# Softmax gradient with a one-hot label: single rows in four buffers against blocks of two rows in three

## The chip, the cores and the metric

The kernel runs on one core of a Trainium2 chip; the other cores stand idle. The metric is the device time of one execution in microseconds. Before the change it is 1255.14 us, the median of 3 runs (1254.55 to 1255.56).

The core's engines that matter here are the Vector engine (DVE), ScalarE (ACT), GpSimd (POOL) and SyncE (SP). ScalarE and SyncE also issue transfers; each has a hardware queue of its own, and all transfers run on the same 16 DMA engines.

## The reference

Logits are 8 x 1024 rows of 8192 fp32 values, labels one integer for each row. The output has the shape of the logits: the softmax of each row, less 1 at the place of its label.

```python
logits_max = np.max(logits, axis=-1, keepdims=True)
exp_logits = np.exp(logits - logits_max)
softmax = exp_logits / np.sum(exp_logits, axis=-1, keepdims=True)
...
one_hot[batch_idx, seq_idx, labels] = 1.0
return (softmax - one_hot).astype(np.float32)
```

Everything is read once and written once: 268 MB in and 268 MB out.

## The kernel before

The 8192 rows are cut into 64 row tiles of 128 rows, one row on each partition, 32 KB of fp32 a row. One loop runs over the row tiles, unrolled in Python, and a scheduler orders the instructions on each engine and places the waits. A tile goes through these steps:

- L47: SyncE's queue loads the row tile (4.19 MB) into one of the four buffers of the pool `io`. The load of row tile t+4 waits until the store of row tile t has landed, because it takes the same buffer.
- L50 and L57: GpSimd's queue loads 128 labels, and the Vector engine casts them to fp32.
- L61: ScalarE computes the exponential into a bf16 tile and, in the same instruction, the sum of each row. No row maximum is taken away first; the exponential of the plain logit is used.
- L71: the Vector engine takes the reciprocal of the sum.
- L74: it compares a table of column numbers (`iota_pv`, int16, made once at L41) with the label and multiplies by the sum. The result, bf16, overwrites the first half of the logits' buffer, which the exponential has read.
- L83: it subtracts that from the exponential, in bf16.
- L85: it multiplies by the reciprocal and writes fp32 back into the logits' buffer.
- L87: ScalarE's queue stores the buffer.

Nothing but the four buffers, two bf16 tiles and the order on each queue ties one row tile to the next.

Of the kernel before, what the change touches and what calls it, by code (L numbers as in the profile page):

```python
# [1 line left out]

# [4 lines left out]

P = 128


@with_exitstack
def kernel(
    ctx: ExitStack,
    tc: tile.TileContext,
    logits: bass.AP,
    labels: bass.AP,
    out: bass.AP,
):
    nc = tc.nc  # L20
    fp32 = mybir.dt.float32
    bf16 = mybir.dt.bfloat16
    i16 = mybir.dt.int16

    logits_nv = logits.flatten_outer_dims()
    out_nv = out.flatten_outer_dims()
    labels_n = labels
    while len(labels_n.shape) > 1:
        labels_n = labels_n.rearrange("a b ... -> (a b) ...")

    N, V = logits_nv.shape
    assert N % P == 0, f"N={N} must be a multiple of {P}"
    n_tiles = N // P

    const_pool = ctx.enter_context(tc.tile_pool(name="const", bufs=1))
    io_pool = ctx.enter_context(tc.tile_pool(name="io", bufs=4))
    work_pool = ctx.enter_context(tc.tile_pool(name="work", bufs=2))
    stats_pool = ctx.enter_context(tc.tile_pool(name="stats", bufs=4))

    iota_pv = const_pool.tile([P, V], i16)  # L40
    nc.gpsimd.iota(iota_pv[:, :], [[1, V]], channel_multiplier=0)  # L41

    for ti in range(n_tiles):
        rs = ti * P

        logits_tile = io_pool.tile([P, V], fp32, tag="io")
        nc.sync.dma_start(out=logits_tile[:], in_=logits_nv[rs : rs + P, :])  # L47

        labels_tile = stats_pool.tile([P, 1], labels_n.dtype, tag="labels")
        nc.gpsimd.dma_start(out=labels_tile[:], in_=labels_n[rs : rs + P, None])  # L50

        labels_f32 = stats_pool.tile([P, 1], fp32, tag="labels_f32")
        if mybir.dt.size(labels_n.dtype) == 8:
            labels_i32 = labels_tile.bitcast(mybir.dt.int32)[:, :1]
        else:
            labels_i32 = labels_tile[:]
        nc.vector.tensor_copy(out=labels_f32[:], in_=labels_i32)  # L57

        exp_bf = work_pool.tile([P, V], bf16, tag="exp")
        sum_f32 = stats_pool.tile([P, 1], fp32, tag="sum")  # L60
        nc.scalar.activation(  # L61
            out=exp_bf[:],
            in_=logits_tile[:],
            func=mybir.ActivationFunctionType.Exp,
            bias=0.0,
            scale=1.0,
            accum_out=sum_f32[:],
        )

        recip_sum = stats_pool.tile([P, 1], fp32, tag="recip")  # L70
        nc.vector.reciprocal(out=recip_sum[:], in_=sum_f32[:])  # L71

        ohts_bf = logits_tile.bitcast(bf16)[:, :V]
        nc.vector.tensor_scalar(  # L74
            out=ohts_bf,
            in0=iota_pv[:, :],
            scalar1=labels_f32[:],
            scalar2=sum_f32[:],
            op0=mybir.AluOpType.is_equal,
            op1=mybir.AluOpType.mult,  # L80
        )

        nc.vector.tensor_sub(out=exp_bf[:], in0=exp_bf[:], in1=ohts_bf)  # L83

        nc.vector.tensor_scalar_mul(out=logits_tile[:], in0=exp_bf[:], scalar1=recip_sum[:])  # L85

        nc.scalar.dma_start(out=out_nv[rs : rs + P, :], in_=logits_tile[:])  # L87


# [1 line left out]
_INS = ['logits', 'labels']  # L91
_OUTS = [((8, 1024, 8192), 'float32')]


# [23 lines left out]
```

The softmax here doesn't subtract the row's maximum and nothing guards it: scores larger than these inputs give would overflow.

## Time and profile before

| What | Value |
|---|---|
| Device time, median of 3 runs | 1255.14 us |
| Span of the profiled execution | 1252.6 us |
| Vector engine busy | 732.6 us (58%) |
| ScalarE busy | 457.0 us (36%) |
| GpSimd busy | 253.0 us (20%) |
| Queue of the loads, share of 16 DMA engines | 49.8% |
| Queue of the stores, share of 16 DMA engines | 49.6% |
| Queue of the labels, share of 16 DMA engines | 0.1% |
| Bytes moved, mean rate | 537.01 MB, 429 GB/s |

The span runs from the first to the last instruction of the program in the profiled execution; the device time of the runs lies some 2.5 us above it. Busy times are sums over an engine's own instructions, and instructions that issue a transfer aren't counted as busy. The share of a queue is the time that its packets took, against 16 engines over the whole span. A row of the groups names line, engine, operation, output and input with shapes and count, and then gives total busy time, mean duration in ns, and the idle time of the engine ahead of these instructions with what ended it. In the row of 40 digits each digit stands for one fortieth of the span, and 9 is 90% or more.

### The profile page before, as it was taken

The numbers are of one execution on the slowest core, as the hardware profiler recorded it, in microseconds if no ns is written. First come the engines' busy times: TensorE is split into PE (matmuls) and PEld (weight loads), VectorE is DVE, ScalarE is ACT, GpSimd is POOL, SyncE is SP. The second block draws the span as 40 slices with busy tenths as digits, with TensorE's granted clock in tenths as the row PEclk, the third lists the DMA queues.
The fourth block names the chain that finished last, engine by engine and source line by source line (L and its number), as shares of the span: only waits on it lengthen the run. The fifth ranks groups of instructions, "written<-read, shape, count | busy, mean of one in ns | idle before, by whom it ended". The sixth has DMA issues, their size and how long they took to land.

```text
span 1252.6 us, 992 instructions
## 1 busy us (share of the span) xinstructions
DVE 732.6 (58%) x320; ACT 457.0 (36%) x129; POOL 253.0 (20%) x69
## 2 busy tenths in 40 slices
DVE  3764655746647556465574664755646556465573
ACT  4424244243342433423424334243342432423422
POOL 5322212212122122221221212212222122100000
DMA  9999999999999999999999999999999999999997
GB/s 400 421 435 434 433 428 430 433 436 433 435 430 432 431 433 433 434 434 432 429 432 435 431 434 433 431 432 432 434 433 434 433 429 432 432 434 435 434 433 311
DMA packets 20487, 537.01 MB, mean 429 GB/s; under 512 B 4096, under 2 KB 4096, under 8 KB 4096
## 3 DMA queue, kind: packets, MB, share of 16 engines
q1 hardware_dynamic: 9216, 268.44, 49.8%
q10 hardware_dynamic: 9216, 268.44, 49.6%
q0 software_dynamic: 2048, 0.07, 0.1%
q14 instruction: 7, 0.06, 0.0%
HBM read 268.50 MB, written 268.44 MB: 429 GB/s over the span
## 4 chain that ended last, share of the span: by engine, by line
DMA 71%; DVE 17%; issue 8%; ACT 1%; POOL 1%; ACTq 0%; SPq 0%; PEldq 0%
DMA out_dram<-logits_tile 38%; DMA logits_tile<-in_logits_dram 32%; DVE logits_tile L85 7%; DVE exp_bf L83 7%; DVE logits_tile L74 4%; ACT exp_bf L61 1%; DMA labels_tile<-in_labels_dram 1%; POOL iota_pv L41 1%; ACTq L87 0%; POOL labels_tile L50 0%; DVE labels_f L57 0%; DVE recip_sum L71 0%; SPq L47 0%; ACTq L61 0%; PEldq L113 0%
## 5 line engine op out<-in xcount | busy, mean ns | idle before, releaser
L61 ACT ACTIVATE exp_bf<-logits_tile 128x8192 bf16<-128x8192 f32 x64 | 449.8, 7029 | 771.3 <-DMA logits_tile<-in_logits_dram 757.8
L50 POOL DMA_DIRECT2D labels_tile<-in_labels_dram x64 | 245.9, 3843 | 832.1 <-DVE labels_f L57 830.1
L71 DVE RECIPROCAL recip_sum<-sum_f 128x1 f32<-128x1 f32 x64 | 10.5, 163 | 485.1 <-ACT exp_bf L61 485.1
L85 DVE TENSOR_SCALAR logits_tile<-exp_bf,recip_sum 128x8192 f32<-128x8192 bf16 x64 | 287.1, 4486 | 0.1
L83 DVE TENSOR_TENSOR exp_bf<-exp_bf,logits_tile 128x8192 bf16<-128x8192 bf16 x64 | 283.2, 4425 | 2.2
L74 DVE TENSOR_SCALAR logits_tile<-iota_pv,labels_f,sum_f 128x8192 bf16<-128x8192 int16 x64 | 154.3, 2412 | 0.3 <-issue 0.3
L57 DVE CAST labels_f<-labels_tile 128x1 f32<-128x1 int32 x64 | 9.4, 147 | 20.2 <-DMA labels_tile<-in_labels_dram 20.2
L61 ACT ACTIVATION_READ_ACCUMULATOR exp_bf<-logits_tile 128x1 f32 x64 | 11.9, 186 | 0.0
L41 POOL IOTA iota_pv<- 128x8192 int16 x1 | 6.9, 6944 | 0.4 <-PEq L113 0.4
L61 ACT ACT_TABLE_LOAD x1 | 1.3, 1283 | 0.7 <-PEq L102 0.7
L102 POOL MEMSET const-float32-0.0<- 128x1 f32 x1 | 0.1, 99 | 0.2 <-issue 0.2
L102 POOL MEMSET const-bfloat16-1.0<- 128x1 bf16 x1 | 0.1, 102 | 0.0
L102 POOL MEMSET const-uint8-127<- 128x1 uint8 x1 | 0.1, 102 | 0.0
L102 POOL MEMSET const-float32-1.0<- 128x1 f32 x1 | 0.1, 99 | 0.0
## 6 DMA issues: line engine op xcount, KB each, us to landing
logits_tile<-in_logits_dram SPq DMA_DIRECT2D x64, 4096.0 KB, 27.2
out_dram<-logits_tile ACTq DMA_DIRECT2D x64, 4096.0 KB, 31.3
labels_tile<-in_labels_dram POOLq DMA_DIRECT2D x64, 1.0 KB, 12.7
```

The costliest lines, as they stand in the source:

```text
L41: nc.gpsimd.iota(iota_pv[:, :], [[1, V]], channel_multiplier=0)
L50: nc.gpsimd.dma_start(out=labels_tile[:], in_=labels_n[rs : rs + P, None])
L57: nc.vector.tensor_copy(out=labels_f32[:], in_=labels_i32)
L61: nc.scalar.activation(out=exp_bf[:], in_=logits_tile[:], func=mybir.ActivationFunctionType.Exp, bias=0.0, scale=1.0, accum_out=sum_f32[:],)
L71: nc.vector.reciprocal(out=recip_sum[:], in_=sum_f32[:])
L74: nc.vector.tensor_scalar(out=ohts_bf, in0=iota_pv[:, :], scalar1=labels_f32[:], scalar2=sum_f32[:], op0=mybir.AluOpType.is_equal, op1=myb ...
L83: nc.vector.tensor_sub(out=exp_bf[:], in0=exp_bf[:], in1=ohts_bf)
L85: nc.vector.tensor_scalar_mul(out=logits_tile[:], in0=exp_bf[:], scalar1=recip_sum[:])
L102: nc = _bacc.Bacc("TRN2", target_bir_lowering=False, num_devices=1)
```

## The change

The kernel is written anew around blocks of two neighbouring rows for each partition. Partition p of block b holds rows 256b + 2p and 256b + 2p + 1, which lie side by side in memory, so that a partition's part of a block is one run of 64 KB.

- `SLOTS` is 3 and `G`, the rows of a block on each partition, is 2. Three buffers of a block each (8.39 MB, 64 KB on each partition) replace four buffers of a row tile and the two bf16 tiles. All steps work in place in fp32.
- A block moves as one load and one store. The first and the last block are loaded row by row, and the first three and the last two are stored row by row (`BY_ROW_IN`, `BY_ROW_OUT`).
- The labels of all rows are loaded once, cast, and transposed through the tensor engine into one column for each row tile, once for each half of the vocabulary.
- The row maximum is computed (`row_max`) and goes into the exponential as its bias.
- The multiplication by the reciprocal moves to ScalarE (`normalize`, two halves), and compare and subtract are one Vector instruction for each half (`subtract`).
- The order is written out by hand: in the pass of row t the Vector engine takes the reciprocal of t, the maximum of row t+1 and then the subtraction of row t; ScalarE takes the exponential of t, issues the store of row t−1 (for a block, after its second row), and then normalizes t.

The diff, cut to its core:

```diff
-    io_pool = ctx.enter_context(tc.tile_pool(name="io", bufs=4))
-    work_pool = ctx.enter_context(tc.tile_pool(name="work", bufs=2))
+    io = ctx.enter_context(tc.tile_pool(name="io", bufs=SLOTS))
+    ctx.enter_context(tc.manual_schedule())
...
+    x_b = x_nv.rearrange("(b p j) v -> b p j v", p=P, j=G)
+    o_b = o_nv.rearrange("(b p j) v -> b p j v", p=P, j=G)
...
+    lab_raw = const.tile([B, G * P], labels.dtype)
+    nc.scalar.dma_start(out=lab_raw[:], in_=lab_bp)
...
+    for j in range(G):
+        nc.vector.tensor_copy(out=lab_f[:, j, :], in_=lab32[:, j, :, 0])
+        nc.tensor.transpose(out=lab_ps[:, j, :], in_=lab_f[:, j, :], identity=ident[:])
+    for c in range(C):
+        nc.vector.tensor_scalar_add(out=lab[:, c], in0=lab_ps[:], scalar1=float(-c * HALF))
...
+    def load(b):
+        x = io.tile([P, G, V], fp32, tag="x", name="x")
+        if b in BY_ROW_IN:
+            for j in range(G):
+                nc.sync.dma_start(out=x[:, j, :], in_=x_b[b, :, j, :])
+        else:
+            nc.sync.dma_start(out=x[:], in_=x_b[b])
+        return x
+    def row_max(x):
...
+        nc.vector.tensor_reduce(out=m[:], in_=x[:], axis=mybir.AxisListType.X, op=Alu.max, negate=True)
...
+    def exponent(x, m):
...
+        nc.scalar.activation(out=x[:], in_=x[:], func=Act.Exp, bias=m[:], scale=1.0, accum_out=s[:])
...
+    def normalize(x, r):
+        for c in range(C):
+            xc = x[:, c * HALF : (c + 1) * HALF]
+            nc.scalar.activation(out=xc, in_=xc, func=Act.Copy, bias=0.0, scale=r[:])
+    def subtract(t, x):
+        for c in range(C):
+            xc = x[:, c * HALF : (c + 1) * HALF]
+            nc.vector.scalar_tensor_tensor(
+                out=xc, in0=iota[:], scalar=lab[:, c, t % G, t // G : t // G + 1], in1=xc,
+                op0=Alu.is_equal, op1=Alu.subtract, reverse1=True,
+            )
+    def store(t):
+        b, j = divmod(t, G)
+        if b in BY_ROW_OUT:
+            nc.scalar.dma_start(out=o_b[b, :, j, :], in_=blocks[b][:, j, :])
+        elif j == G - 1:
+            nc.scalar.dma_start(out=o_b[b], in_=blocks[b][:])
+    BY_ROW_IN = (0, B - 1)
+    BY_ROW_OUT = (0, 1, 2, B - 2, B - 1)
...
+    m = row_max(row(0))
+    for t in range(T):
+        s = exponent(row(t), m)
+        r = inverse(s)
+        if t + 1 < T:
+            m = row_max(row(t + 1))
+        if t > 0:
+            store(t - 1)
+        normalize(row(t), r)
+        subtract(t, row(t))
+    store(T - 1)
```

## The prediction

> **What bounds the kernel now.** I read the page from its top: span and DMA row first, then the waits of ScalarE and of SyncE's DMA queue, then the costs of single instructions, and last the places where the DMA engines stand still.
>
> ```profile
> span 1252.6 us, 992 instructions
> DVE 732.6 (58%) x320; ACT 457.0 (36%) x129; POOL 253.0 (20%) x69
> DMA  9999999999999999999999999999999999999997
> GB/s 400 421 435 434 433 428 430 433 436 433 435 430 432 431 433 433 434 434 432 429 432 435 431 434 433 431 432 432 434 433 434 433 429 432 432 434 435 434 433 311
> ```
>
> The engines have room, the 16 DMA engines have none: 537 MB at about 433 GB/s are 1240 of the 1252.6 us. The waits say the same:
>
> ```profile
> ACT exp_bf L61 <- DMA logits_tile<-in_logits_dram: 757.8, 62, 19.2
> SPq L47 <- DMA out_dram<-logits_tile: 1169.6, 60, 50.2
> ```
>
> ScalarE waits for loads, and the load queue waits for stores to free one of the four buffers. That second wait costs nothing now: in the chain of waits a load is issued the moment a store lands, while another load or store still keeps the DMA engines busy.
>
> ```profile
> 619.70 31.99 DMA out_dram<-logits_tile
> 651.69 0.02 SPq L47
> 651.74 26.60 DMA logits_tile<-in_logits_dram
> ```
>
> Prices of single instructions, from the groups:
>
> ```profile
> L61 ACT ACTIVATE exp_bf<-logits_tile 128x8192 bf16<-128x8192 f32 x64 | 449.8, 7029 | 771.3 <-DMA logits_tile<-in_logits_dram 757.8
> L83 DVE TENSOR_TENSOR exp_bf<-exp_bf,logits_tile 128x8192 bf16<-128x8192 bf16 x64 | 283.2, 4425 | 2.2
> ```
>
> Prices of a transfer with nothing beside it. In the stretches (length, busy time of DVE, ACT and POOL, clock, DMA share, GB/s) no byte moves before 1.60 us although the first load is issued at 0.75; loads alone run at 420 to 423, loads and stores mixed at 433; and near the end the DMA share falls to 0.41 and 0.75.
>
> ```profile
> 1.20:1.60 0.40, 0.00 (x0) 0.40 (x1) 0.40 (x1) 1.00 0.00 0
> 1.60:2.00 0.40, 0.00 (x0) 0.40 (x1) 0.40 (x1) 1.00 3.27 901
> 20.00:30.00 10.00, 9.36 (x6) 6.89 (x3) 4.17 (x2) 1.00 1.01 420
> 160.00:320.00 160.00, 94.43 (x43) 58.97 (x18) 34.27 (x8) 1.00 1.00 433
> 1230.00:1240.00 10.00, 9.93 (x3) 0.00 (x0) 0.00 (x0) 1.00 0.41 177
> 1240.00:1253.00 13.00, 0.51 (x1) 0.00 (x0) 0.00 (x0) 1.00 0.75 323
> ```
>
> Issue to landing (min/median/max), first of the loads, then of the stores; the two minima are the first load and the last store, which had the engines to themselves:
>
> ```profile
> DMA to landing us min/median/max: 12.3/27.2/48.4
> DMA to landing us min/median/max: 11.1/31.3/33.5
> ```
>
> A row tile is 4.19 MB, 9.7 us at 433 GB/s. So a lone load costs 2.6 us on top of its bytes and a lone store 1.4.
>
> **What the Trainium skill says.** "DMA: Bandwidth & Descriptors", section Anatomy of one DMA, gives each transfer a fixed cost of about 2.0 us, mostly the receipt of the last write, and says that waits are served by the issuing sequencer, not by the DMA engines; the 2.6 and 1.4 us agree in size. Its section Queues, rings and completion order says that each DMA engine takes turns between queues packet by packet, so a load and a store that run together share about evenly; the equal packet shares of the two queues here (49.8% and 49.6%) fit. Its section Where 436 GB/s comes from puts the ceiling at 435.2 GB/s; 433 in the trace is 0.5% below, which bounds what longer runs can give. "VectorE: DVE Perf Modes", section The perf-mode tier table, has a reduction at one element a cycle in any type and a two-input operation on fp32 likewise.
>
> **The change, part by part.**
>
> *Traffic.* Bytes stay. 64 KB runs for 32 KB ones and one label load for 64: between 0 and 1240 × 0.5% = 6 us less; I take 2.
>
> *Vector engine.* It loses L74, L83, L85, and L57's casts, and gains a row maximum over 8192 fp32 and two fused compare-and-subtract over 4096 (int16 and fp32 in). The trace has neither. L83 makes 8192 elements at two a cycle in 4.425 us; at one a cycle 4096 elements cost the same, 4.43, and 8192 cost 8.69 (L83 plus 4096 more cycles at 0.96 GHz, 4.27 us). A row: 8.69 + 2 × 4.43 + 0.16 (reciprocal) = 17.7 us, a block of two rows 35.4, against 38.75 for a block's traffic (16.78 MB at 433). Below: the fused operation can't be cheaper than two elements a cycle, 2.3 us; above, two cycles an element, 8.7. One a cycle is taken because both forms read two inputs.
>
> *ScalarE.* The exponential stays at 7.03 + 0.19 for the accumulator; new are two copies with scale over 4096, half of 7.03 plus about 0.2, so 3.6 to 3.7 each. A row is 14.6 us, hidden under the Vector engine's 17.7. Setup (iota, transpose of labels) lies under the first load; first Vector work is due at 13 us.
>
> *Buffers and waits: the part that decides.* Three blocks of 8.39 MB replace four tiles of 4.19 MB, and except in the first and last blocks each moves as one load and one store. Load b+3 waits for the whole store b. And the Vector engine's order is maximum(t+1) before subtract(t). So the store of block b, behind subtract of its second row, stands behind the maximum of the first row of block b+1, and that behind the landing of load b+1. From load b+1 landing to the first byte of store b: 8.69 + 8.86 + about 0.3 (reciprocal, hand-overs) + 0.34 issue + about 0.8 (the last store is issued at 1240.54, bytes flow from about 1241.3) = 19.0 us.
>
> At the moment store b−1 lands, what else can move? Store b is up to 19 us away. Load b+1 started before store b−1 and shared with it, so it is done. Load b+2 is the one that waited for this very landing. Nothing is left, and the engines stand still for a gap g. One period: gap g; load alone for a; both for c; store alone for s. Each moves 8.39 MB (19.4 us alone): a + c/2 = 19.4 = s + c/2, so a = s; landing to next store: s + g + a = 19.0. With g = 2.4, a = s = 8.3, c = 22.2, period 41.2 = 38.75 + g. The Vector engine (35.4) is not late; it waits 5.8 us a block for loads.
>
> The size of g: last byte to landing is 1.4 − 0.8 = 0.6; issue to data at full rate is a load's 2.6 − 0.6 = 2.0; together 2.6. If the first load's 2.0 holds one-time cost and a load starts like a store, 0.8, then g = 1.4. I take 2.4, since the slow first packets of a load from rest should recur.
>
> *One direction alone.* In 8.3 us of each period loads run by themselves, at 420 to 423: 2.6% or 0.2 us a block, up to 7 us in all; a store alone isn't measured in the middle. I take 4.
>
> *Start.* Row 0 lands near 12.5, maximum to 21.8, exponential to 29, maximum of row 1 and subtract of row 0 to 47. The first three loads (25.2 MB) cover until about 58, so before the first gap only the 2.0 us ahead of the first data are lost, as now.
>
> *Tail.* Now 10 × 0.59 + 13 × 0.25 = 9 us idle in the last 23. After: the last four rows are stored singly, 9.7 us of bytes each 17.7 us of Vector work, with the last row shorter; I keep 9 (5 to 15).
>
> *Sum.* 1240.2 − 2 + 4 + 2.0 + 29 loads × 2.4 (69.6) + 9 = 1322.8 us span. The runs shown have a median 2.5 us above the profiled span, so 1325 us.
>
> **Rivals.**
>
> *A weaker gap:* g between 0.2 and 1.4, if part of the restart is hidden, gives 1261 to 1296. For it: first-packet cost has been seen just once. Against: landing, queue wake and issue can't overlap with the transfer they follow.
>
> *No gap (not slower).* If stores win over loads on the shared engines, a store lands while the next load still runs, and load follows load. Then the sum loses 69.6: 1255.8, and with the full 6 us from longer runs and none of the 4 for single direction, 1248. It decides only where g is practically nothing, or below (1255.1 − 1248) / 29 = 0.25 us a block with that full gain. For it: now the same wait is hidden. Against: with 19 us from landing to store and 19.4 us for a store alone, load after load leaves no room for a store that must also share.
>
> *Vector engine bound.* If the fused operation takes over (41.2 − 17.4 − 0.3)/4 = 5.9 us, the Vector engine sets the period; at 6.5 us it is 64 × 21.9 = 1400, plus 12 ahead and 25 behind, about 1437. Against: L83's rate with two inputs.
>
> **How the numbers follow.** The gap of 1.4 to 2.9: 0.75, giving 1296 to 1340, with the spread of tail and single direction 1288 to 1348. Weaker gap: 0.09. No gap: 0.11, of it 0.07 faster, 0.04 within 0.2% (about what a measurement of this kernel can tell from no change). Vector bound: 0.05. So faster 0.07, same 0.04, slower 0.89. Range 1275 to 1348: it leaves out the no-gap case, the Vector bound and the low end of the weak gap.
>
> **What would show it.** Right: a mean rate near 407 GB/s; the Vector engine's maximum waiting for loads about 5 us in every other row; in stretches of 1 us a hole in DMA between each store's landing and the next load's first bytes, one per 41 us; SyncE's queue waiting for stores with nothing else in flight. Wrong: 430 GB/s in the middle slices, a fused operation far from 4.4 us, or a store issued before the next block's load has landed.

## The result and the profile after

The changed kernel takes 1362.41 us, the median of 4 runs (1360.13 to 1364.21), against 1254.86 us for the kernel before: a ratio of 1.0855 (95% interval 1.084 to 1.0871). It is slower by 107.6 us. The forecast was slower, 1325 us, and the range ended at 1348.

The head of the page of the changed kernel, with span, busy time of the engines, rate by fortieths of the span and queue shares:

```profile
span 1360.3 us, 777 instructions
PE 0.4 (0%) x2; PEld 0.3 (0%) x2; DVE 1119.6 (82%) x260; ACT 930.7 (68%) x257; POOL 4.0 (0%) x7
DMA  9999999999999999999999998999999999999997
GB/s 405 426 389 447 401 401 401 370 393 403 407 401 370 401 401 401 401 370 401 401 401 401 370 399 376 428 391 380 370 401 432 370 372 397 403 401 401 372 429 309
q1 hardware_dynamic: 4896, 268.44, 49.5%
q10 hardware_dynamic: 5376, 268.50, 45.6%
```

The bytes are the same and the rate is lower, from the fifth slice on in every one: 370 to 432 where some 433 stood. The row of digits hides it, since a hole of 2 us in a slice of 34 us still reads 9. The Vector engine has 1119.6 us of work in 1360.3 and isn't the bound. The prices of its new instructions came out as worked out (group rows as before):

```profile
L81 DVE TENSOR_REDUCE m<-x 128x1 f32<-128x8192 f32 x64 | 555.2, 8675 | 209.9 <-DMA x<-in_logits_dram 209.9
L102 DVE SCALAR_TENSOR_TENSOR x<-iota,lab,x 128x4096 f32<-128x4096 int16 x128 | 567.9, 4480 | 4.1 <-ACT x L97 4.1
L97 ACT ACTIVATE x<-x,r 128x4096 f32<-128x4096 f32 x128 | 467.7, 3700 | 115.2 <-DVE r L91 115.2
```

The maximum waits 209.9 us for loads. The chain of waits, in order of time, has the whole loop in it (start, length, what):

```profile
600.27 30.15 DMA out_dram<-x
630.42 0.02 SPq L76
630.45 0.03 issue
630.48 37.62 DMA x<-in_logits_dram
668.09 0.03 issue
668.12 0.02 DVEq L81
668.14 0.04 issue
668.19 8.69 DVE m L81
676.87 7.32 DVE x L102 x2
```

A store lands at 630.42; a load that waited for it is issued at 630.48 and lands at 668.1; the maximum and the subtraction follow, and the next store of this chain is issued at 685.69. What the engines do around that landing is seen in stretches of 1 us (length, busy PE, PE weights, DVE, ACT and POOL, clock, DMA share, GB/s; a packet counts where it begins, so a 64 KB packet of 2.4 us reads as a burst):

```profile
629.00:630.00 1.00, 0.00 (x0) 0.00 (x0) 1.00 (x1) 1.00 (x1) 0.00 (x0) 1.00 0.01 0
630.00:631.00 1.00, 0.00 (x0) 0.00 (x0) 1.00 (x1) 1.00 (x1) 0.00 (x0) 1.00 0.00 0
631.00:632.00 1.00, 0.00 (x0) 0.00 (x0) 1.00 (x2) 1.00 (x1) 0.00 (x0) 1.00 2.68 918
```

No packet begins between 629 and 631, the last of the store's semaphore writes apart, and load bytes start after 631. That is the hole which the prediction put there. In the packet records of the trace the last store packet ends at 630.07 and the first load packet begins at 631.42; between 200 and 1100 us there are 22 such holes of 1.3 to 1.9 us with nothing in flight. But holes are only half of the loss. One long stretch of the middle, 200 to 1100 us, first of the kernel before (busy DVE, ACT, POOL), then of the changed one (busy PE, PE weights, DVE, ACT, POOL, as in all kernels that follow):

```profile
200.00:1100.00 900.00, 532.96 (x233) 328.37 (x94) 197.06 (x46) 1.00 1.00 433
```

```profile
200.00:1100.00 900.00, 0.00 (x0) 0.00 (x0) 731.90 (x169) 609.93 (x168) 0.00 (x0) 1.00 0.95 393
```

The share fell from 1.00 to 0.95: 45 us of standstill in 900. The rate fell further, to 393. At a share of 0.95 the rate while at work is 393 / 0.95 = 414, not 433: the packets themselves take longer, which is another 0.95 × 900 × (1 − 414/433) = 38 us. With loads issued every 42.5 us (588.01, 630.48 and 672.97 are three in a row), this stretch holds 21 blocks; a block loses 2.1 us to standstill and 1.8 us to slow packets, 3.9 us in all.

The packet records say which packets are slow. The 64 KB packets of stores take 2.42 us throughout; those of loads have a mean of 2.63 us, and the excess lies in two places. The first packets of a load that starts from rest take some 0.7 us more. And when a store begins beside a running load, the 16 or so load packets then in flight take 3.4 to 3.9 us (medians of the 21 starts between 200 and 1100 us).

A price can be put on each start. Here and below it is the time that the packets in flight at the start took beyond their usual 2.418 us (64 KB) or 1.213 us (32 KB), divided among 16 engines; a start counts where its queue had nothing in flight for more than 2.5 us before. In the stretch of 900 us, 21 loads that start from rest cost 0.65 us each, and 21 stores that start beside a load 1.2 us each (1.0 to 1.4). Together these are 39 us, all but 0.4 us of the excess.

### The profile page after: what moved, and what is told of

Its sections match the earlier page's. It is cut to its first block, busy times and chain, and to the rows that moved or that the text cites. A ratio compares the mean times of both kernels' runs of the same rounds, so it can differ in the third digit from the quotient of the medians.

```text
span 1360.3 us, 777 instructions
## 1 busy us (share of the span) xinstructions
PE 0.4 (0%) x2; PEld 0.3 (0%) x2; DVE 1119.6 (82%) x260; ACT 930.7 (68%) x257; POOL 4.0 (0%) x7
## 4 chain that ended last, share of the span: by engine, by line
DMA 68%; DVE 28%; issue 2%; ACT 1%; DVEq 0%; SPq 0%; ACTq 0%
DMA x<-in_logits_dram 39%; DMA out_dram<-x 28%; DVE m L81 15%; DVE x L102 13%; ACT x L86 1%; DVEq L162 0%; ACT x L97 0%; DVE r L91 0%; SPq L76 0%; DVEq L81 0%; ACTq L110 0%; DVEq L102 0%
## 5 line engine op out<-in xcount | busy, mean ns | idle before, releaser
L81 DVE TENSOR_REDUCE m<-x 128x1 f32<-128x8192 f32 x64 | 555.2, 8675 | 209.9 <-DMA x<-in_logits_dram 209.9
L86 ACT ACTIVATE x<-x,m 128x8192 f32<-128x8192 f32 x64 | 455.8, 7122 | 284.0 <-DVE m L81 284.0
L102 DVE SCALAR_TENSOR_TENSOR x<-iota,lab,x 128x4096 f32<-128x4096 int16 x128 | 567.9, 4480 | 4.1 <-ACT x L97 4.1
L97 ACT ACTIVATE x<-x,r 128x4096 f32<-128x4096 f32 x128 | 467.7, 3700 | 115.2 <-DVE r L91 115.2
L91 DVE RECIPROCAL r<-s 128x1 f32<-128x1 f32 x64 | 10.2, 160 | 7.3 <-ACT x L86 7.3
L86 ACT ACTIVATION_READ_ACCUMULATOR x<-x,m 128x1 f32 x64 | 11.9, 187 | 0.0
L52 POOL IOTA iota<- 128x4096 int16 x1 | 3.5, 3541 | 0.4 <-POOLq L151 0.4
```

The source lines that it names most:

```text
L52: nc.gpsimd.iota(iota[:], [[1, HALF]], base=0, channel_multiplier=0)
L81: nc.vector.tensor_reduce(out=m[:], in_=x[:], axis=mybir.AxisListType.X, op=Alu.max, negate=True)
L86: nc.scalar.activation(out=x[:], in_=x[:], func=Act.Exp, bias=m[:], scale=1.0, accum_out=s[:])
L91: nc.vector.reciprocal(out=r[:], in_=s[:])
L97: nc.scalar.activation(out=xc, in_=xc, func=Act.Copy, bias=0.0, scale=r[:])
L102: nc.vector.scalar_tensor_tensor(out=xc, in0=iota[:], scalar=lab[:, c, t % G, t // G : t // G + 1], in1=xc, op0=Alu.is_equal, op1=Alu.subt ...
```

## The experiments

Theory A: larger transfers in fewer buffers let the queues run dry once a block, and a queue that runs dry costs twice, in standstill and in slow packets at the restart. Rivals: B, 64 KB runs are slower in themselves; C, the Vector engine's chain of maximum and subtract sets the time; D, which comes up with the last three kernels, the slow packets are an effect of the hole before them. Diffs are against the changed kernel unless another is named.

### 32 KB runs in blocks of the same size

```diff
-    x_b = x_nv.rearrange("(b p j) v -> b p j v", p=P, j=G)
-    o_b = o_nv.rearrange("(b p j) v -> b p j v", p=P, j=G)
+    x_b = x_nv.rearrange("(b j p) v -> b p j v", p=P, j=G)
+    o_b = o_nv.rearrange("(b j p) v -> b p j v", p=P, j=G)
...
-    lab32 = lab_raw[:].bitcast(i32).rearrange("b (p j s) -> b j p s", j=G, s=step)
+    lab32 = lab_raw[:].bitcast(i32).rearrange("b (j p s) -> b j p s", j=G, s=step)
```

> Blocks as in the changed kernel, one load and one store each, but partition p of block b holds rows 256b + p and 256b + 128 + p, so that every run is 32 KB. Theory A (both queues run dry once a block and pay for the restart: about 2.0 us of standstill, 0.7 us of slow first load packets and 1.2 us of slow load packets when a store begins): run length plays no part, 1350 to 1365 us. Theory B (64 KB runs are slower in themselves; loads took 2632 ns a packet against 2418 for stores): the 50 us of slow load packets go, 1305 to 1320 us. Should the slow packet at the start of a store be a share of a packet, its cost halves and A gives about 1345.

Measured: 1347.57 us (ratio 1.0731, 1.0715 to 1.0747). In the middle:

```profile
200.00:1100.00 900.00, 0.00 (x0) 0.00 (x0) 752.67 (x173) 624.46 (x173) 0.00 (x0) 1.00 0.95 397
```

Standstill is unchanged, and 397 / 0.95 = 418 while at work is only a little better than 414. Half the run length takes 15 of 107.6 us away. B would have taken some 50, so it falls. A's first range, in which run length plays no part, was missed too; its variant, that a store's start costs a share of a packet, said about 1345 and came close. The packet records agree: a store that starts beside a load costs 0.61 us here, half of the 1.2 us with 64 KB runs, and a load from rest 0.54.

### Stores row by row, loads in blocks of 64 KB runs

```diff
-    BY_ROW_OUT = (0, 1, 2, B - 2, B - 1)
+    BY_ROW_OUT = tuple(range(B))
```

> All stores row by row, loads in blocks as in the changed kernel. Theory A: a row's store takes the engines for under 20 us while stores come every 17 to 20 us, so the store queue is hardly ever empty when the last row of a block lands; standstill and restarts nearly vanish, 1250 to 1262 us, with fewer than 5 holes in DMA. Theory B: loads still move in 64 KB runs and stay slow, 1300 us or more. Theory C (the Vector engine's chain of maximum and subtract from landing to store sets the time): the chain is unchanged, 1350 to 1365 us.

Measured: 1261.1 us (ratio 1.0043, 1.0026 to 1.006). One line, and 101 of the 107.6 us are gone, with the same engine work, the same three buffers and loads still in blocks:

```profile
200.00:1100.00 900.00, 0.00 (x0) 0.00 (x0) 814.03 (x186) 672.05 (x186) 0.00 (x0) 1.00 1.00 433
```

No standstill, no slow packets, 433 GB/s with loads in 64 KB runs. B and C fall here together: the loads' runs are the same, the chain from maximum to subtract is the same. The line does change one more thing, since a store by row has runs of 32 KB; with 32 KB runs and block transfers, above, the time was 1347.57 us, so it isn't the run length of the stores that brings the gain. What is left over the kernel before is the end of the kernel:

```profile
1200.00:1230.00 30.00, 0.00 (x0) 0.00 (x0) 30.00 (x8) 25.25 (x7) 0.00 (x0) 1.00 0.90 388
1230.00:1240.00 10.00, 0.00 (x0) 0.00 (x0) 5.92 (x4) 8.04 (x4) 0.00 (x0) 1.00 0.48 206
1240.00:1250.00 10.00, 0.00 (x0) 0.00 (x0) 8.37 (x2) 3.06 (x1) 0.00 (x0) 1.00 0.61 265
1250.00:1260.60 10.60, 0.00 (x0) 0.00 (x0) 0.00 (x0) 0.00 (x0) 0.00 (x0) 1.00 0.80 346
```

These idle 3.0 + 5.2 + 3.9 + 2.1 = 14 us, 5 more than the 9 of the kernel before, while the last rows leave one by one at the Vector engine's pace (stores issued at 1200.47, 1217.92 and 1235.36).

### Loads row by row, stores in blocks

```diff
-    BY_ROW_IN = (0, B - 1)
+    BY_ROW_IN = tuple(range(B))
```

> All loads row by row, stores in blocks as in the changed kernel. Theory A: the first row of a block lands half a block earlier, which moves the chain to the store forward by some 10 us, but the next load still waits for a whole store; standstill shrinks while the slow packets at the start of a store (1.2 us a block) and the restart of loads stay, 1280 to 1310 us. Theory B: loads are in 32 KB runs, the slow load packets go, about 1310 us. Theory C: the chain begins earlier, 1260 to 1290 us.

Measured: 1326.86 us (ratio 1.0572, 1.0545 to 1.0598), above what A expected. The middle:

```profile
200.00:1100.00 900.00, 0.00 (x0) 0.00 (x0) 769.77 (x177) 638.88 (x177) 0.00 (x0) 1.00 0.98 410
```

Standstill shrank as expected, from 5% to 2%. The slow packets shrank less: 410 / 0.98 = 418 while at work is a loss of some 30 us in the 900, where the changed kernel loses 38. All three miss the number (A ended at 1310, B said about 1310, C ended at 1290), and the run before has ruled out B and C. The load's size is worth 36 us by itself, the store's 101.

### Loads and stores row by row

```diff
-    BY_ROW_IN = (0, B - 1)
-    BY_ROW_OUT = (0, 1, 2, B - 2, B - 1)
+    BY_ROW_IN = tuple(range(B))
+    BY_ROW_OUT = tuple(range(B))
```

> Loads and stores row by row, three block buffers of two rows; nothing in the transfers is larger than in the kernel before. Theory A: as with stores by row alone (1261 us), the store queue hardly runs dry; loads by row add nothing to the middle but make the first row of a block land earlier, 1248 to 1262 us. Theory B (64 KB runs carry a price of their own) has nothing left to charge here either, and would expect it well below the kernel with stores by row alone, by 5 us or more.

Measured: 1257.69 us (ratio 1.0028, 1.0015 to 1.004). The middle:

```profile
200.00:1100.00 900.00, 0.00 (x0) 0.00 (x0) 815.26 (x187) 676.03 (x188) 0.00 (x0) 1.00 1.00 433
```

That is 3.4 us below stores by row alone, under the 5 us that B would have wanted; the intervals of the two ratios overlap, so even this gain isn't sure. All runs are 32 KB here, as with the 32 KB runs in blocks (1347.57 us). Between these two kernels the size of the transfers differs and the length of the runs doesn't, and the 90 us between them go with the size.

### The row maximum left out

```diff
     def row_max(x):
-        m = stats.tile([P, 1], fp32, tag="m", name="m")
-        nc.vector.tensor_reduce(out=m[:], in_=x[:], axis=mybir.AxisListType.X, op=Alu.max, negate=True)
-        return m
+        return None
...
-        nc.scalar.activation(out=x[:], in_=x[:], func=Act.Exp, bias=m[:], scale=1.0, accum_out=s[:])
+        nc.scalar.activation(out=x[:], in_=x[:], func=Act.Exp, bias=0.0, scale=1.0, accum_out=s[:])
```

> The row maximum is left out (bias 0, as in the kernel before); the order of the rest and all transfers stay. It takes 8.67 us off the Vector engine for each row. Theory A: store b still stands behind the landing of load b+1 (now through ScalarE, which takes the exponential of the next row before it issues the store), so a hole stays after each store: 1330 to 1350 us. Theory C: nearly half of the Vector engine's work is gone and with it the waits, 1250 to 1275 us. Theory B: 1310 us or more.

Measured: 1311.62 us (ratio 1.0447, 1.0427 to 1.0468), below A's 1330 and far above C's 1275. B's "1310 us or more" allows it, but B has fallen with stores by row.

```profile
PE 0.4 (0%) x2; PEld 0.3 (0%) x2; DVE 579.6 (44%) x196; ACT 921.2 (70%) x257; POOL 4.0 (0%) x7
200.00:1100.00 900.00, 0.00 (x0) 0.00 (x0) 397.94 (x132) 631.67 (x177) 0.00 (x0) 1.00 0.99 410
```

540 us of Vector work are gone and only 51 us of time. A was wrong about the hole: the share is 0.99, so the store now comes early enough to leave none. The loss over the kernel before, 56 us, is nearly all slow packets: 410 / 0.99 = 414 while at work, the very rate of the changed kernel. This run parts the two halves of the loss: standstill can go alone and the slow packets stay. In the packet records there is no moment between 200 and 1100 us with nothing in flight, yet 11 stores that start beside a load cost 1.4 us each and 11 loads that start beside a store 1.8 us each. Rival D, which needs a hole, falls here.

### The row maximum left out and stores row by row

```diff
+    (row_max returns None and the exponential has bias 0.0, as above)
-    BY_ROW_OUT = (0, 1, 2, B - 2, B - 1)
+    BY_ROW_OUT = tuple(range(B))
```

> Without the row maximum and with all stores row by row, loads in blocks. Without the maximum alone the time was 1312 us with the DMA engines at a share of 0.99 in the middle, so that nearly all of its loss is slow packets and not standstill. If slow packets come from queues that run dry (theory A), smaller stores take them away: 1243 to 1256 us, 433 GB/s in the middle. If they come from the restart of block loads beside a running store, they stay: 1280 us or more.

Measured: 1249.59 us (ratio 0.9953, 0.9936 to 0.9969).

```profile
200.00:1100.00 900.00, 0.00 (x0) 0.00 (x0) 418.26 (x140) 668.80 (x188) 0.00 (x0) 1.00 1.00 434
```

The slow packets go with the large stores, beside unchanged block loads. In the packet records of this kernel, as with stores by row alone, the load queue still runs empty 29 times while a store runs, and those restarts cost next to nothing: 0.02 us each for the 24 between 200 and 1100 us, against the 1.8 us beside block stores. So it isn't every restart that is slow. The store queue in these two kernels hardly runs empty, one to three times in that stretch.

### Single rows in six buffers, and in four

```diff
-SLOTS = 3
-G = 2
+SLOTS = 6
+G = 1
```

> The changed kernel with one row a partition in a block (G = 1) and six buffers of 4.19 MB: the same memory, the same instructions on the Vector engine and on ScalarE, transfers of the size of the kernel before, 32 KB runs. Theory A: with six buffers two more loads are always free to run, neither queue runs dry, 1244 to 1254 us. Theory C (the Vector engine's chain): unchanged against the changed kernel, 1340 us or more.

Measured: 1248.39 us (ratio 0.9946, 0.993 to 0.9963), 0.5% below the kernel before. The engines' work and the memory are those of the changed kernel; the transfers are 4.19 MB and there are twice as many buffers. The middle:

```profile
200.00:1100.00 900.00, 0.00 (x0) 0.00 (x0) 825.28 (x189) 683.67 (x189) 0.00 (x0) 1.00 1.00 433
```

That is the rate of the kernel before; the gain is at the end, where the DMA share stays at 0.97 and 1.00 from 1220 to 1240 us, against 0.41 for the kernel before from 1230 to 1240:

```profile
1220.00:1230.00 10.00, 0.00 (x0) 0.00 (x0) 6.75 (x2) 6.82 (x2) 0.00 (x0) 1.00 0.97 419
1230.00:1240.00 10.00, 0.00 (x0) 0.00 (x0) 2.13 (x1) 0.00 (x0) 0.00 (x0) 1.00 1.00 429
```

The same with four buffers (`SLOTS = 4`):

> As with six buffers of one row a partition, but with four, as many as in the kernel before. Maximum, order and instructions as in the changed kernel. Theory A: transfers are small, but with four buffers and 19 us from the landing of a load to the store of the row before it, too few transfers are free at any one time; both queues run dry again, 1295 to 1330 us, with tens of holes. If only the size of a transfer mattered, it would be the 1248 us of six buffers.

Measured: 1319.54 us (ratio 1.0519, 1.0489 to 1.0549), and in the middle:

```profile
200.00:1100.00 900.00, 0.00 (x0) 0.00 (x0) 779.17 (x179) 646.33 (x180) 0.00 (x0) 1.00 0.99 414
```

Small transfers alone don't save it. The kernel before has four buffers as well and 433 GB/s; with the maximum ahead of the exponential, and the next maximum ahead of the subtraction, a buffer should be held longer, and four are then too few. That reason is argued and no run shows it. Most of this loss, too, is packets at 414 / 0.99 = 418 GB/s, not standstill, and the tens of holes that were expected didn't come (five, of 0.3 to 0.7 us). In the packet records 20 loads and 24 stores start on an empty queue beside the other queue between 200 and 1100 us, with six buffers none. They cost 0.6 and 0.5 us on average, from nothing to 1.2 us, although no transfer is larger than a row. So block stores aren't the condition for a slow restart.

The six buffers with the last row stored in two halves:

```diff
-    store(T - 1)
+    for c in range(C):
+        cs = slice(c * HALF, (c + 1) * HALF)
+        nc.scalar.dma_start(out=o_b[B - 1, :, 0, cs], in_=row(T - 1)[:, cs])
```

> As with six buffers of one row a partition (1248 us), with the last row stored in two halves, the first as soon as it is subtracted. In the middle nothing changes; at the end half a row tile (4.8 us at 433 GB/s) goes out under the last subtraction of 4.48 us: 1242 to 1246 us.

Measured: 1248.26 us (ratio 0.9948, 0.9935 to 0.9962), no change from 1248.39. The expectation took an idle end for granted, and with six buffers there is little left to fill.

### Transfers alone

Three kernels without any computation were meant to measure a store's start by itself. The first:

```diff
+    xs = [const.tile([P, G, V], fp32, name=f"x{i}") for i in range(2)]
+    st = const.tile([P, G, V], fp32, name="st")
+    nc.vector.memset(st[:], 0.0)
+    for b in range(B + 8):
+        nc.sync.dma_start(out=xs[b % 2][:], in_=x_b[b % B])
+    for b in range(B):
+        nc.scalar.dma_start(out=o_b[b], in_=st[:])
```

> Transfers alone, no computation: 40 loads of a block of 8.39 MB into two buffers in turn (always one waiting behind the one that runs) and 32 stores of a block of zeros, all issued as early as the queue takes them, so that neither queue runs dry until the stores are done. 72 blocks at 433 GB/s are 1395 us; all theories: 1390 to 1415 us, no load packet above 2.6 us once both run.

Measured: 1411.09 us, one run. The second adds, behind each store, a write of one column of `st`, so that the next store waits for the landing of this one:

```diff
         nc.scalar.dma_start(out=o_b[b], in_=st[:])
+        nc.vector.memset(st[:, 0, 0:1], 0.0)
```

> As the probe with full queues, but each store waits until the store before it has landed, so that the store queue runs dry 31 times while loads run on. The DMA engines always have loads to move. Theory A (a store that begins on an empty queue costs 1.2 us of everybody's time): 31 x 1.2 = 37 us more than with full queues, and load packets of 3 to 4 us at each start. Rival D (the slow packets in the changed kernel come from the hole before them, not from the start of a store): the same time within 5 us.

Measured: 1503.38 us, one run, 92 us more. The third stores single rows, each waiting likewise:

> As the probe with a dry store queue, but with stores of a row tile, 64 of 4.19 MB in place of 32 of 8.39 MB, each waiting for the landing of the one before. Theory A with a price for each start: 63 x 1.2 = 76 us more than with full queues. If the price goes with the size of the packet (32 KB here), half of that, 38 us. Rival D: the same time as with full queues within 5 us.

Measured: 1482.21 us, one run, 71 us more. These totals mean less than they seem to, because loads came to wait as well, though they share no data with the stores. SyncE's queue in the kernel with waiting block stores:

```profile
SPq L54 <- DMA out_dram<-st: 365.2, 7, 103.2
```

Loads that wait for stores were not meant to be there, and why they wait isn't shown. Only a stretch without such a wait can be used, 200 to 600 us, first with full queues, then with waiting block stores (busy DVE and POOL, clock, share, GB/s):

```profile
200.00:600.00 400.00, 0.00 (x0) 0.00 (x0) 1.00 1.00 432
```

```profile
200.00:600.00 400.00, 0.47 (x8) 0.00 (x0) 1.00 1.00 425
```

Eight stores begin in it, as the eight small writes count, and the rate is 425 for 432 at a share of 1.00: 400 × (1 − 425/432) = 6.5 us go to slow packets. That would be 0.8 us a start, but the packet records don't put the loss there. The packets in flight at seven of the eight starts lost 0.03 to 0.4 us, those at the eighth, at 473.5 us, 1.4 us; together 2.7 us of the 7.4 us that all packets of the stretch lost. The rest is scattered between the starts. So a price of 1.2 us for every start, which theory A wanted, isn't shown here: without computation a start can be slow, and mostly isn't. The third kernel settles nothing about the size of a store.

## Why the prediction was right in direction and wrong in size

- *What bounds the kernel, prices of instructions:* right. 4.43 was 4.48, 8.69 was 8.68, 3.6 to 3.7 was 3.70 us; the Vector engine isn't the bound, and cutting half its work (no row maximum) leaves 1312 us.
- *The wait that decides:* right. Load b+3 behind the landing of the whole store b, and store b behind the landing of load b+1, leave a hole after each store; 629 to 631 us shows one. From landing to the issue of the next store, 668.1 to 685.69, are 17.6 us, where the working has 17.9 (8.69 + 8.86 + 0.3). With stores by row the holes and 101 us are gone.
- *The size of g, 2.4 us:* about right as it was meant, a standstill and slow first packets of a load. Standstill measures 2.1 us a block, and the first load packets 0.65 us more in the packet records, 2.7 in all.
- *The period, 38.75 us and g, with 4 us in all for "one direction alone":* this is the step that failed. Outside the gap it charged a block only for its bytes, and put a store's start beside a running load at nothing; the 4 us were meant for loads that run by themselves, from the rate of the first loads of the kernel before. In the packet records each store that starts beside a load costs 1.2 us, by load packets of 3.4 to 3.9 us for 2.4. Together standstill and slow packets measure 3.9 us a block, against (69.6 + 4) / 29 = 2.5 in the sum. The missing 1.4 us × 29 = 41 us carry 1325 to 1366, and 1362.4 was measured; 1.2 us × 27 block stores = 32 us of it are the stores' starts, and most of the rest is g at 2.7 for 2.4.
- *Sharing of the queues:* packets in turn were right, though the equal shares of 49.8% and 49.6% don't show it, since both queues move the same bytes whatever their order. Stores by row show it: where both queues run (stretches of 4 us with at least 8 packets of each), 2681 load packets of 64 KB stand beside 2897 store packets of 32 KB. What sharing costs when a queue starts again, the kernel before couldn't show: neither of its queues runs empty for more than 2.5 us between 60 us and its last store. The kernel without the maximum shows it best: share 0.99, yet 410 GB/s.
- *Even periods:* wrong in form only. Two blocks alternate: stores are issued at 600.27, 635.96 and 685.69, 35.7 and 49.7 us apart. Between 200 and 1100 us the maximum waits 14 to 16 us for every other block and at most 1.2 us for the ones between, rather than 5.8 us for each.
- *Start, tail:* right; the tail idles 9.5 us (shares 0.62, 0.61 and 0.83 from 1330 us on), where 9 was kept.
- *Traffic:* the gain of 2 us from 64 KB runs can't be seen; 433 with loads in 64 KB runs and with 32 KB runs throughout.
- *Rivals:* a weaker gap, no gap and a Vector bound were each refuted by the same lines. The case that came true, a larger loss by the named mechanism, was given only the width of the tail.

What stays open is what sets the price of a restart. With 64 KB packets on both queues a store beside a load cost 1.2 to 1.4 us and a load beside a store 1.8; with 32 KB packets on both, 0.6 in blocks, and from nothing to 1.2 us in four buffers of single rows; a block load beside a row's store costs 0.02. Neither the size of the transfer nor that of the packet orders all of these, and how the 16 engines stand to each other at that moment wasn't varied.

## What to carry to other kernels

Count transfers, not bytes of buffer: in a kernel bound by DMA, each queue needs something ready to run at the moment when another transfer lands, and the size of a store is the grain in which buffers come free. Halving the stores, or using six small buffers for three large ones in the same memory, was worth 101 and 114 us here. Runs of 64 KB for 32 KB brought no rate that could be measured with full queues, and cost 15 us where the queues ran empty. Look at share and rate of the DMA engines together in a long stretch: a share under 1 is standstill, and a rate that is low by more than the share is slow packets, which the busy rows don't show.

## What the runs showed of the hardware that was not expected

A DMA share near 1.00 doesn't mean the full rate. With the same bytes, 32 KB runs, row transfers and queues, six buffers move 433 GB/s at a share of 1.00 and four buffers 414 at 0.99. The packet records tell them apart by queues that run empty and start again beside the other: none between 200 and 1100 us against 44.

Two queues that both have work take turns by packets, not by bytes: 2681 load packets of 64 KB beside 2897 store packets of 32 KB with stores by row, so that the loads got 1.85 times the bytes.
